# Moving the gate and spill stores to another issuing engine, laying value tiles over finished scratch memory, and starting 92 instead of 79 expert tiles before the gates are done

## The chip, the cores and the metric

The kernel runs on one core of a Trainium2 chip. The metric is the time of one execution on the device, in microseconds (us). PE is the matrix engine (TensorE), DVE is VectorE, ACT is ScalarE, POOL is GpSimd, and SP is SyncE, which here only issues transfers (DMA). Each engine works through its own list of instructions in order; an instruction that waits holds up all that stand behind it on that engine.

## What is computed

The reference is one decoder layer: gated token mixers, and then an expert network (PEER) that takes more than two thirds of the time. Only the second half is touched by the change:

```
def peer(xn, wq, subkeys, u_tab, v_tab):          # 512 tokens, 8 heads, 16 picks a head
    q = (xn @ wq).reshape(bsz, s, PEER_HEADS, 2, PEER_HALF)
    sub = jnp.einsum('bshpd,hpnd->bshpn', q, subkeys)
    s_top, i_top = lax.top_k(sub, PEER_TOPK)       # 16 best of 128 row keys and of 128 column keys
    ...
    best, pos = lax.top_k(cand, PEER_TOPK)         # 16 best of their 256 sums
    expert = jnp.take_along_axis(cand_idx, pos, axis=-1)
    gate = jax.nn.softmax(best, axis=-1)
    ...
    a = gelu(einsum('td,ted->te', xb, u_tab[eb]))
    return einsum('te,ted->td', (gb * a), v_tab[eb])
```

There are 128 x 128 = 16384 experts, each one row of 1024 numbers in the table U and one in the table V.

## The kernel before

The first third of the program (to about 540 us) is the token mixers, the projection to `q` and the search for the best keys. What follows treats the 512 tokens in two ways.

**Dense, for tokens 0 to 383** (three blocks of 128). All 16384 experts are computed, in 128 tiles of 128 experts. An *expert tile* j (`expert_in`) loads a 512 KB tile of U (`wraw`), splits it into a high part (`whi`, cast on ACT) and a low part (`wlo`, subtraction on DVE), multiplies both on PE with the tokens (24 matmuls, `pa`), and applies gelu on ACT. The result (128 experts x 384 tokens, `act`) needs the gates before it can be used. The *gates* are a table of 128 x 384 x 128 numbers, nearly all zero: `choose(b)` finds picks and weights on DVE, then 24 rounds build one-hot tiles on DVE (`jb`, `ib`, `o1`, `o2`) and multiply them on PE (`pg`, 768 products in all), ACT copies the products to `ch`, and 24 stores of 1 MB write them to the memory `gd`. After that the *value loop* runs over j = 0 to 127: a value tile of V is loaded and split like a U tile (`load_w(vt[j], wv, 4)`; four raw tiles, two high and two low ones), a block of gates `gg` (1.5 MB for eight j) is read back from `gd`, DVE multiplies it with `act` (`pr`), ACT and DVE split the product (`ph`, `pl`), and 18 matmuls add to the six sums `y`. Expert tiles that were not done before run between the value tiles.

**Sparse, for tokens 384 to 511.** 128 gathers of U rows (`sparse_in`: POOL gathers, DVE reduces to `dots`) and 128 gathers of V rows (`sparse_out`: DVE adds to `h2l`). Three gather buffers are shared.

Expert tiles do not depend on the gates, so `ahead` runs the first `AHEAD` of them while DVE works on keys and gates. Tiles 0 to 27 stay in SBUF; tiles 28 to AHEAD - 1 are written to the memory `ad` (`actd`, 192 KB each, two buffers) and read back in the value loop. `load_w` has three raw tiles for U and issues its loads on SP. In the kernel before all stores are issued on SP too, and so stand in one list with the loads.

The order on each engine is not that of the code. A scheduler arranges the instructions by its own model before the program is built, and the engines then keep that order whatever the real times are. A pool that is opened after another was closed lies over the closed one's memory, and its first writers wait, tile by tile, for the last users of what lay there.

Of the kernel before, what the change touches and what calls it, by code (L numbers as in the profile page):

```python
# [9 lines left out]
F32 = mybir.dt.float32  # L10
F32R = mybir.dt.float32r
F16 = mybir.dt.float16
# [8 lines left out]
P = 128  # L21
# [39 lines left out]
def kernel(ctx: ExitStack, tc: tile.TileContext, x, pos, cst, wtok, wsm, wcol, wkv, spt,  # L61
                             wab, wo, wq, skt, g1b, g2b, u_rows, ut, v_rows, out, dbg=None):
    nc = tc.nc
    V, G, A, T, SY = nc.vector, nc.gpsimd, nc.scalar, nc.tensor, nc.sync
# [16 lines left out]
    def load_w(src, wp=wp, raws=RAW):  # L81
        raw = wp.tile([P, D], F32, name="wraw", tag="wraw", bufs=raws)
        hi = wp.tile([P, D], F32R, name="whi", tag="whi")
        lo = wp.tile([P, D], F32R, name="wlo", tag="wlo")
        SY.dma_start(raw, src)
        A.copy(hi, raw)  # L86
        V.tensor_tensor(lo, raw, hi.bitcast(F32), ALU.subtract)  # L87
        return hi, lo
# [54 lines left out]
    with ExitStack() as c1:  # L143
# [39 lines left out]
        with tc.tile_pool(name="xin", bufs=4, reuse_waits="tile") as xp:  # L183
# [43 lines left out]
            with tc.tile_pool(name="rp", bufs=1) as rp:  # L227
# [38 lines left out]
                for k, p2 in ((a1, 9), (a2, 20)):  # L266
# [4 lines left out]
                    t = tmp()  # L271
# [351 lines left out]
    TO = 8  # L623
    NCH = ND // TC
    JG = 8
    AHEAD = 79
    KEPT = 28
    EARLY = 2
    GS = 2.0 ** 15
# [12 lines left out]
    def expert_in(j):  # L642

        hi, lo = load_w(ut[j])
        ps = psa.tile([P, S], F32, name="pa", tag="pa")
        expert_mm(ps, hi, lo, 0, ND)
        if KEPT <= j < AHEAD:
            a = spill.tile([P, ND], F32, name="actd")
            A.activation(a, ps[:, :ND], AF.Gelu_apprx_tanh)  # L649
            SY.dma_start(ad[j - KEPT], a)  # L650
            return None
        a = stash.tile([P, ND], F32, name="act")
        A.activation(a, ps[:, :ND], AF.Gelu_apprx_tanh)
        return a
# [31 lines left out]
    with ExitStack() as c2:  # L686
# [6 lines left out]
        iota = kp.tile([P, P], F16, name="iota")  # L693
        V.tensor_copy(iota, iota_i)
        it16 = iota[:, :PK]
        iob = kp.tile([P, TO // 4, P, 4], F16, name="iob")
        V.tensor_copy(iob, iota.unsqueeze(1).unsqueeze(3).to_broadcast([P, TO // 4, P, 4]))

        order = [NB - 1] + list(range(NB - 1))
        top_s = [kp.tile([P, PH, 2, PK], F32, name=f"top_s{b}") for b in range(NB)]  # L700
# [33 lines left out]
                        top16(top_s[b][:, h, p, :], top_i[b][:, h, p, :], subs[p][:, b * P:(b + 1) * P])  # L734

        ks = c2.enter_context(tc.tile_pool(name="ks", bufs=2, reuse_waits="tile"))
        chp = c2.enter_context(tc.tile_pool(name="chp", bufs=2, reuse_waits="tile"))
        oh = c2.enter_context(tc.tile_pool(name="oh", bufs=2, reuse_waits="tile"))

# [60 lines left out]
        for b in range(NB - 1):  # L800
            ahead(2)
            tr = []
            for n, src in enumerate(choose(b)):
                pt = sm.tile([P, S], F32, name="pgt", tag="sm")
                T.transpose(pt[:, :P], src, ident)
                t = ks.tile([P, P], F32 if n == 2 else F16, name=f"tr{n}")
                A.activation(t, pt[:, :P], AF.Copy, scale=GS if n == 2 else 1.0)
                tr.append(t)
            jT, iT, gT = tr[1], tr[0], tr[2]
            ghi = ks.tile([P, P], F16, name="ghi")  # L810
            V.tensor_copy(ghi, gT)
            glo = ks.tile([P, P], F16, name="glo")
            V.tensor_tensor(glo, gT, ghi, ALU.subtract)
            for cc in range(P // TC):
                ch = chp.tile([P, P, TC], F32, name="ch")
                for to in range(0, TC, TO):
                    t0 = cc * TC + to

                    ahead(1)

                    def over(a):
                        return (a[:, t0:t0 + TO].rearrange("p (g u) -> p g u", u=4).unsqueeze(2)
                                .to_broadcast([P, TO // 4, P, 4]))

                    jb, ib, o1, o2 = (oh.tile([P, TO // 4, P, 4], F16, name=n) for n in ("jb", "ib", "o1", "o2"))
                    V.tensor_tensor(jb, iob, over(jT), ALU.is_equal)
                    V.tensor_tensor(ib, iob, over(iT), ALU.is_equal)
                    V.tensor_tensor(o1, ib, over(ghi), ALU.mult)  # L828
                    V.tensor_tensor(o2, ib, over(glo), ALU.mult)
                    for t4 in range(0, TO, 4):  # L830
                        pg = gp.tile([P, 4, P], F32, name="pg")
                        for u in range(4):
                            for o in (o1, o2):
                                T.matmul(pg[:, u, :], jb[:, t4 // 4, :, u], o[:, t4 // 4, :, u], start=o is o1,  # L834
                                         stop=o is o2)
                        A.activation(ch[:, :, to + t4:to + t4 + 4].rearrange("p i t -> p t i"), pg, AF.Copy,  # L836
                                     scale=1.0 / GS)
                SY.dma_start(gd[:, b * (P // TC) + cc], ch)

        ahead(P)  # L840

    with ExitStack() as c3:
        yp = c3.enter_context(tc.tile_pool(name="yp", bufs=1, space=PSUM))
        gr = c3.enter_context(tc.tile_pool(name="gr", bufs=2, reuse_waits="tile"))
        wv = c3.enter_context(tc.tile_pool(name="wv", bufs=2, reuse_waits="tile"))
        cp = c3.enter_context(tc.tile_pool(name="cp", bufs=3, reuse_waits="tile"))
        ys = [[yp.tile([P, 512], F32, name=f"y{b}_{hf}") for hf in range(2)] for b in range(NB - 1)]
        vt = v_rows.rearrange("(i j) d -> i j d", j=P)
# [3 lines left out]
        def feed():  # L852

            done[0] += 1
            while done[1] < n_todo and done[1] * n_load < n_todo * done[0]:
                f, s = todo[done[1]]
                f(s)
                done[1] += 1

        for j in range(P):  # L860
            if j % JG == 0:
                gt = gr.tile([P, NCH, JG, TC], F32, name="gg", tag="gg")
                SY.dma_start(gt, gd[:, :, j:j + JG, :])
                if j + JG == P:
                    hr = gr.tile([P, NB - 1, D], F32, name="hr", tag="gg")
                    SY.dma_start(hr, hd)
            room = max(KEPT - 5 - max(0, KEPT - j), 0) + max(0, j - AHEAD)
            while len(acts) < min(P, AHEAD + min(room, (P - AHEAD) * (j + 1) // (P - 4))):
                acts.append(expert_in(len(acts)))
                feed()  # L870
            if acts[j] is None:
                acts[j] = stash.tile([P, ND], F32, name="act")
                SY.dma_start(acts[j], ad[j - KEPT])
            hi, lo = load_w(vt[j], wv, 4)
            pr = cp.tile([P, ND], F32, name="pr", bufs=2)
            V.tensor_tensor(pr.rearrange("p (c t) -> p c t", c=NCH), acts[j].rearrange("p (c t) -> p c t", c=NCH),
                            gt[:, :, j % JG, :], ALU.mult)
            ph = cp.tile([P, ND], F32R, name="ph")
            pl = cp.tile([P, ND], F32R, name="pl")
            A.copy(ph, pr)  # L880
            V.tensor_tensor(pl, pr, ph.bitcast(F32), ALU.subtract)  # L881
            for b in range(NB - 1):
                bs = slice(b * P, (b + 1) * P)
                for hf in range(2):
                    ds = slice(hf * 512, (hf + 1) * 512)
                    with tc.issue_after(last_mm.ins) if j == P - 1 and (b or hf) else nullcontext():
                        last_mm = mm3(ys[b][hf], ph[:, bs], pl[:, bs], hi[:, ds], lo[:, ds], j == 0, j == P - 1)
            feed()
# [75 lines left out]
```

## Time and profile before

| | us |
|---|---|
| median of three runs | 1670.01 (1667.72 to 1675.47) |
| the profiled execution, its own time | 1667.96 |
| span of its profile | 1666.2 |
| PE busy | 1604.0 (96%) |
| DVE busy | 1274.0 (76%) |
| ACT busy | 647.7 (39%) |

The span runs from the first to the last instruction in the profile; the other 1.8 us lie around it. Busy time counts work alone: an engine that only issues a transfer is not counted as busy for it. "Idle" is always the idle time of one engine, and costs something only where that engine is the one that the end waits for. The share of 96% is an average over the program; the slices and windows below show where the rest is.

### The profile page before, as it was taken

Reading aid. Unit: us, or ns where it says so; the run is one execution under the profiler, and the core shown is the slowest. Engines: PE = TensorE matmul, PEld = TensorE weight load, DVE = VectorE, ACT = ScalarE, POOL = GpSimd, SP = SyncE. Lnnn points to the kernel's source line nnn. Section 1 sums busy time; section 2 is a strip of 40 time slices with the busy share of each in tenths; the row PEclk is TensorE's granted clock in tenths of the full one; section 3 lists DMA queues with packets and bytes.
Section 4 is the critical chain, followed back from the end, with each engine's and each line's share of the span. In section 5 each row is a group of like instructions: output and inputs, shape, how many; then the busy total and the mean of one; then the engine's idle time right before and its main releaser. Section 6 shows DMA issues by size and latency. Waiting matters only on the chain.

```text
span 1666.2 us, 22533 instructions
## 1 busy us (share of the span) xinstructions
PE 1604.0 (96%) x8173; PEld 1400.8 (84%) x8173; DVE 1274.0 (76%) x2670; ACT 647.7 (39%) x954; POOL 357.2 (21%) x280
## 2 busy tenths in 40 slices
PE   8999999999999999999995499999999999999999
PEld 6777768888899999999994488888888888988887
DVE  5599955459999998888888588878788788874543
ACT  5453333332344344555555233333333333333332
POOL 0010000000001442222222233434434234430000
PEclk9999999999999999999995699999999999999999
DMA  5212233222224898889878999999999989985432
GB/s 209 76 51 76 89 136 117 89 102 89 77 102 159 299 323 295 316 278 332 300 280 290 313 314 334 342 350 338 338 344 341 371 309 323 326 317 183 152 126 77
DMA packets 154351, 386.74 MB, mean 232 GB/s; under 512 B 12288, under 2 KB 74496, under 8 KB 150656
## 3 DMA queue, kind: packets, MB, share of 16 engines
q1 hardware_dynamic: 117376, 251.07, 42.6%
q0 software_dynamic: 36864, 134.23, 23.2%
q8 instruction: 64, 1.05, 0.2%
q14 instruction: 47, 0.39, 0.1%
HBM read 346.40 MB, written 38.86 MB: 231 GB/s over the span
## 4 chain that ended last, share of the span: by engine, by line
PE 65%; DVE 12%; DMA 12%; issue 7%; POOL 3%; ACT 1%; SPq 0%; POOLq 0%; DVEq 0%; ACTq 0%
PE pa L93 6%; PE pa L91 6%; PE pa L92 6%; PE y L92 6%; PE y L91 6%; PE y L93 6%; DMA gt<-in_v_rows,eid 5%; PE pg L834 4%; DVE wlo L87 3%; POOL gt L658 3%; PE pcol L92 2%; PE pcol L91 2%; PE pcol L93 2%; PE pq L92 2%; PE pq L91 2%
## 5 line engine op out<-in xcount | busy, mean ns | idle before, releaser
L86 ACT CAST whi<-wraw 128x1024 fp32r<-128x1024 f32 x320 | 335.0, 1053 | 372.8 <-PE pa L92 129.7
L87 DVE TENSOR_TENSOR wlo<-wraw,whi 128x1024 fp32r<-128x1024 f32 x320 | 389.1, 1218 | 95.2 <-ACT whi L86 90.7
L93 PE MATMUL pa<-hh,wlo 128*128 128x384 f32 (+2 forms) x1040 | 350.5, 338 | 1.9 <-DVE wlo L87 1.9
L91 PE MATMUL pa<-hh,whi 128*128 128x384 f32 (+2 forms) x1040 | 350.0, 337 | 0.7 <-ACT actd L649 0.7
L92 PE MATMUL pa<-hl,whi 128*128 128x384 f32 (+2 forms) x1040 | 349.8, 336 | 0.0
L92 PE MATMUL y<-wlo,ph 128*128 128x512 f32 x768 | 299.9, 391 | 0.4 <-DVE wlo L87 0.4
L93 PE MATMUL y<-whi,pl 128*128 128x512 f32 x768 | 296.6, 391 | 0.0
L658 POOL DMA_INDIRECT gt<-in_u_rows,eid x128 | 167.8, 1311 | 530.2 <-DVE dots L664 328.0
L91 PE MATMUL y<-whi,ph 128*128 128x512 f32 x768 | 239.2, 393 | 27.5 <-ACT whi L86 27.4
L658 POOL DMA_INDIRECT gt<-in_v_rows,eid x128 | 177.1, 1383 | 262.9 <-DVE h2l L673 221.6
L880 ACT CAST ph<-pr 128x384 fp32r<-128x384 f32 x128 | 65.4, 514 | 357.7 <-PE y L92 292.8
L93 PEld LDWEIGHTS pa<-hh,wlo 128*128 128x128 f32 x1040 | 196.9, 189 | 5.6 <-DVE wlo L87 3.4
L91 PEld LDWEIGHTS pa<-hh,whi 128*128 128x128 f32 x1040 | 197.0, 189 | 5.0 <-ACT actd L649 1.4
L92 PEld LDWEIGHTS pa<-hl,whi 128*128 128x128 f32 x1040 | 196.8, 189 | 3.3
L673 DVE SCALAR_TENSOR_TENSOR h2l<-gt,coef,h2l 128x1024 f32<-128x1024 f32 x128 | 164.0, 1281 | 42.7 <-DMA gt<-in_v_rows,eid 41.7
L91 PEld LDWEIGHTS y<-whi,ph 128*128 128x128 f32 x768 | 144.2, 189 | 55.3 <-ACT whi L86 28.1
L664 DVE CUSTOM_DVE_ANT_0 gt<-gt,hn 128x1024 f32<-128x1024 f32 x128 | 155.6, 1218 | 33.0 <-DMA gt<-in_u_rows,eid 32.9
L92 PEld LDWEIGHTS y<-wlo,ph 128*128 128x128 f32 x768 | 144.1, 188 | 30.2 <-DVE wlo L87 0.7
L93 PEld LDWEIGHTS y<-whi,pl 128*128 128x128 f32 x768 | 144.2, 188 | 29.3
L881 DVE TENSOR_TENSOR pl<-pr,ph 128x384 fp32r<-128x384 f32 x128 | 70.5, 554 | 96.7 <-ACT ph L880 94.6
L836 ACT ACTIVATE ch<-pg 128x512 f32<-128x512 f32 x96 | 97.1, 1097 | 69.0 <-PE pg L834 63.2
L834 PE MATMUL pg<-o,jb 128*128 128x128 f16 x768 | 104.6, 296 | 12.4 <-DVE o L828 9.9
(305 smaller groups left out, 1977.4 us busy)
## 6 DMA issues: line engine op xcount, KB each, us to landing
wraw<-in_ut SPq DMA_DIRECT2D x128, 512.0 KB
wraw<-in_v_rows SPq DMA_DIRECT2D x128, 512.0 KB
gd<-ch SPq DMA_DIRECT2D x24, 1024.0 KB
gg<-gd SPq DMA_DIRECT2D x16, 1536.0 KB
wraw<-in_wcol SPq DMA_DIRECT2D x20, 512.0 KB
ad<-actd SPq DMA_DIRECT2D x51, 192.0 KB
act<-ad SPq DMA_DIRECT2D x51, 192.0 KB
wraw<-in_wq SPq DMA_DIRECT2D x16, 512.0 KB
```

Source lines behind the costliest of these rows:

```text
L86: A.copy(hi, raw)
L87: V.tensor_tensor(lo, raw, hi.bitcast(F32), ALU.subtract)
L91: T.matmul(ps, lh, rh, start=start, stop=False)
L92: T.matmul(ps, lh, rl, start=False, stop=False)
L93: return T.matmul(ps, ll, rh, start=False, stop=stop)
L658: G.indirect_dma_start(out=t, out_offset=None, in_=table, in_offset=bass.IndirectOffsetOnAxis(ap=eid[:, s:s + 1], axis=0))
L664: V.tensor_tensor_reduce(out=t, in0=t, in1=hn3, scale=1.0, scalar=0.0, op0=ALU.mult, op1=ALU.add, accum_out=dots[:, s:s + 1])
L673: V.scalar_tensor_tensor(h2l, t, coef[:, s:s + 1], h2l, ALU.mult, ALU.add)
L834: T.matmul(pg[:, u, :], jb[:, t4 // 4, :, u], o[:, t4 // 4, :, u], start=o is o1, stop=o is o2)
L836: A.activation(ch[:, :, to + t4:to + t4 + 4].rearrange("p i t -> p t i"), pg, AF.Copy, scale=1.0 / GS)
L880: A.copy(ph, pr)
L881: V.tensor_tensor(pl, pr, ph.bitcast(F32), ALU.subtract)
```

## The change

Three things are changed. The stores of `gd` and of `ad` are issued by ACT, the engine that wrote what they store, and no longer by SP. The memory is laid out anew: what the 24 rounds still need (`tr`, `ghi`, `glo`, `iob`) moves from the pools `ks` and `kp` to a pool `gs` of its own, and the value pool `wv` is opened ahead of the gate pool `gr`, so that it lies over `kp` and `ks`, which are done when the last `choose` is. The value tiles are loaded by `load_v`, which is called for tiles 0 and 1 ahead of the loop. And `AHEAD` is 92, so that 64 instead of 51 tiles are written to `ad` and read back, and 36 instead of 49 are left for the value loop.

```diff
-    AHEAD = 79
+    AHEAD = 92
...
             A.activation(a, ps[:, :ND], AF.Gelu_apprx_tanh)
-            SY.dma_start(ad[j - KEPT], a)
+            A.dma_start(ad[j - KEPT], a)
...
-        iob = kp.tile([P, TO // 4, P, 4], F16, name="iob")
-        V.tensor_copy(iob, iota.unsqueeze(1).unsqueeze(3).to_broadcast([P, TO // 4, P, 4]))
...
         ks = c2.enter_context(tc.tile_pool(name="ks", bufs=2, reuse_waits="tile"))
+        gs = c2.enter_context(tc.tile_pool(name="gs", bufs=2, reuse_waits="tile"))
+        iob = gs.tile([P, TO // 4, P, 4], F16, name="iob", bufs=1)
+        V.tensor_copy(iob, iota.unsqueeze(1).unsqueeze(3).to_broadcast([P, TO // 4, P, 4]))
...
-                t = ks.tile([P, P], F32 if n == 2 else F16, name=f"tr{n}")
+                t = gs.tile([P, P], F32 if n == 2 else F16, name=f"tr{n}")
...
-            ghi = ks.tile([P, P], F16, name="ghi")
+            ghi = gs.tile([P, P], F16, name="ghi")
...
-            glo = ks.tile([P, P], F16, name="glo")
+            glo = gs.tile([P, P], F16, name="glo")
...
-                SY.dma_start(gd[:, b * (P // TC) + cc], ch)
+                A.dma_start(gd[:, b * (P // TC) + cc], ch)
...
+        wv = c3.enter_context(tc.tile_pool(name="wv", bufs=2, reuse_waits="tile"))
         gr = c3.enter_context(tc.tile_pool(name="gr", bufs=2, reuse_waits="tile"))
-        wv = c3.enter_context(tc.tile_pool(name="wv", bufs=2, reuse_waits="tile"))
...
+        vq = []
+
+        def load_v(n):
+            while len(vq) < min(n, P):
+                vq.append(load_w(vt[len(vq)], wv, 4))
+
+        load_v(2)
         for j in range(P):
...
-            hi, lo = load_w(vt[j], wv, 4)
+            load_v(j + 1)
+            hi, lo = vq[j]
```

What this does to the order is seen at the hand-over from the gates to the value loop. The numbers in the names below are buffer numbers, which the two programs give out differently.

SP, before: the last stores of gates (`gd`), the first block of gates read back (`gg`) and the first value tiles (`in_v_rows`). The loads of U in it are tiles 86 and 87.

```order
L838 DMA gd_3137<-ch_7067 128x2048
L85 DMA wraw_9625<-in_ut 128x1024
L838 DMA gd_3137<-ch_7196 128x2048
L85 DMA wraw_9730<-in_ut 128x1024
L838 DMA gd_3137<-ch_7325 128x2048
L838 DMA gd_3137<-ch_7454 128x2048
L838 DMA gd_3137<-ch_7583 128x2048
L838 DMA gd_3137<-ch_7712 128x2048
L863 DMA gg_8682<-gd_3137 128x24x128
L85 DMA wraw_8684<-in_v_rows 128x1024
L85 DMA wraw_8720<-in_v_rows 128x1024
```

SP, now, at the same place: loads of U tiles 94 to 99 (`wraw_9569` to `wraw_10339`), the first two value tiles, the gates.

```order
L85 DMA wraw_9569<-in_ut 128x1024
L85 DMA wraw_9709<-in_ut 128x1024
L85 DMA wraw_9885<-in_ut 128x1024
L85 DMA wraw_10023<-in_ut 128x1024
L85 DMA wraw_10201<-in_ut 128x1024
L85 DMA wraw_10339<-in_ut 128x1024
L85 DMA wraw_9149<-in_v_rows 128x1024
L85 DMA wraw_9155<-in_v_rows 128x1024
L871 DMA gg_9161<-gd_3137 128x24x128
L85 DMA wraw_9222<-in_v_rows 128x1024
L85 DMA wraw_9255<-in_v_rows 128x1024
```

No store is left on SP, two value tiles stand ahead of `gg`, and all of them stand behind the load of U tile 99.

ACT, before, at the same place: the last copies of gate products, then the first products of the value loop.

```order
L836 ACTIVATE ch_7712<-pg_7755 128x4x128
L836 ACTIVATE ch_7712<-pg_7765 128x4x128
L836 ACTIVATE ch_7712<-pg_7820 128x4x128
L836 ACTIVATE ch_7712<-pg_7830 128x4x128
L880 CAST ph_8692<-pr_8690 128x384
L880 CAST ph_8728<-pr_8726 128x384
L86 CAST whi_8685<-wraw_8684 128x1024
```

ACT, now: the last copies, the stores among them, the casts of U tiles 94 to 97 (`whi_9570` to `whi_10024`), those of value tiles 0 and 1, the first product.

```order
L837 ACTIVATE ch_7715<-pg_7833 128x4x128
L650 DMA ad_3149<-actd_9084 128x384
L839 DMA gd_3137<-ch_7715 128x2048
L86 CAST whi_9570<-wraw_9569 128x1024
L649 ACTIVATE actd_9118<-pa_9093 128x384
L653 ACTIVATE act_9388<-pa_9363 128x384
L650 DMA ad_3149<-actd_9118 128x384
L86 CAST whi_9710<-wraw_9709 128x1024
L86 CAST whi_9886<-wraw_9885 128x1024
L86 CAST whi_10024<-wraw_10023 128x1024
L86 CAST whi_9150<-wraw_9149 128x1024
L86 CAST whi_9156<-wraw_9155 128x1024
```

Before, nothing stood between the last gates and the first product `ph`; now four casts of U tiles and two of value tiles do (`ph` is the next row).

DVE, now: the last low parts of U tiles with reductions of gathered rows (`gt`, the `ISA` rows) between them, then value tiles 0 and 1 and the first product. Before, the rows there were seven such reductions and then `pr`.

```order
L87 TENSOR_TENSOR wlo_9887<-wraw_9885,whi_9886 128x1024
L664 ISA gt_10333,dots_3142<-gt_10333,hn3_2653 128x1024
L664 ISA dots_3142 128x1
L87 TENSOR_TENSOR wlo_10025<-wraw_10023,whi_10024 128x1024
L664 ISA gt_10336,dots_3142<-gt_10336,hn3_2653 128x1024
L664 ISA dots_3142 128x1
L664 ISA gt_10372,dots_3142<-gt_10372,hn3_2653 128x1024
L664 ISA dots_3142 128x1
L87 TENSOR_TENSOR wlo_9151<-wraw_9149,whi_9150 128x1024
L87 TENSOR_TENSOR wlo_9157<-wraw_9155,whi_9156 128x1024
L885 TENSOR_TENSOR pr_9163<-act0_3126,gg_9161 128x384
```

The low part of tile 96, the first row, is what sets free the raw tile that the load of tile 99 fills.

On PE the rows are too alike to be shown, so here are their counts. Before, the last expert tile ahead of the gates' end is number 81 (counted from 0): 24 matmuls, then 176 of the 768 gate products in one stretch, then `y`. Now expert tiles stand between the gate products to their end: after the last product follow the last 20 matmuls of tile 91, tiles 92, 93 and 94 whole, and then `y`.

## Rows read from the trace of the kernel before

**Rows 1.** The page, 40 slices of 41.7 us: busy tenths of PE, granted clock.

```profile
PE   8999999999999999999995499999999999999999
...
PEclk9999999999999999999995699999999999999999
```

**Rows 2.** Busy time by stretch: PE, PEld, DVE, ACT, POOL, clock, DMA share, GB/s.

```profile
600.00:875.50 275.50, 273.59 (x1746) 261.53 (x1745) 234.46 (x349) 141.37 (x176) 75.79 (x57) 0.99 0.86 304
875.50:911.20 35.70, 23.67 (x177) 19.63 (x176) 33.15 (x56) 21.21 (x23) 9.44 (x9) 0.59 0.86 298
911.20:938.20 27.00, 0.02 (x1) 0.02 (x1) 9.50 (x19) 3.22 (x6) 7.80 (x7) 0.50 0.92 318
938.20:944.00 5.80, 5.80 (x17) 5.22 (x18) 4.49 (x6) 2.06 (x4) 0.94 (x1) 0.53 1.00 289
938.20:1500.00 561.80, 560.85 (x2641) 486.54 (x2642) 454.94 (x538) 197.79 (x275) 216.19 (x162) 1.00 0.95 333
1200.00:1300.00 100.00, 100.00 (x466) 85.68 (x465) 80.03 (x90) 34.33 (x47) 39.83 (x26) 1.00 0.99 345
```

**Rows 3.** PE in order of time: start, length, what, idle before.

```profile
869.50 1.95 PE L834 MATMUL pg<-o,jb 128*128 128x128 f16 x15
871.20 0.42 PE L91 MATMUL pa<-hh,whi 128*128 128x384 f32 x1
...
875.47 2.19 PE L834 MATMUL pg<-o,jb 128*128 128x128 f16 x17
...
909.36 1.80 PE L834 MATMUL pg<-o,jb 128*128 128x128 f16 x14 [0.20 <-DVE o L829]
938.18 2.07 PE L91 MATMUL y<-whi,ph 128*128 128x512 f32 x4 [27.02 <-ACT whi L86]
```

**Rows 4.** The chain of work that ended last, at the hand-over: start, length, what.

```profile
910.38 1.96 ACT ch L836 x2
...
912.36 8.03 DMA gd<-ch
...
920.60 0.61 SPq L863
...
921.30 15.68 DMA wraw<-in_v_rows
```

**Rows 5.** DVE and ACT in order of time at the hand-over.

```profile
933.74 1.23 DVE L664 CUSTOM_DVE_ANT_0 gt<-gt,hn 128x1024 f32<-128x1024 f32 x1 [9.66 <-DMA gt<-in_u_rows,eid]
...
934.89 1.02 DVE L876 TENSOR_TENSOR pr<-act,gg 128x384 f32<-128x384 f32 x2
...
935.48 0.98 ACT L880 CAST ph<-pr 128x384 fp32r<-128x384 f32 x2 [23.15 <-DVE pr L876]
```

**Rows 6.** Groups by shape, 700 to 860 us: busy us, mean ns, idle before.

```profile
L664 DVE CUSTOM_DVE_ANT_0 gt<-gt,hn 128x1024 f32<-128x1024 f32 x32 | 39.0, 1218 | 0.0
...
L87 DVE TENSOR_TENSOR wlo<-wraw,whi 128x1024 fp32r<-128x1024 f32 x27 | 33.0, 1222 | 14.5 <-ACT whi L86 14.5
L86 ACT CAST whi<-wraw 128x1024 fp32r<-128x1024 f32 x27 | 28.6, 1059 | 17.5 <-PE pa L92 15.2 <-DVE o L828 1.5 <-DMA wraw<-in_ut 0.7
L828 DVE TENSOR_TENSOR o<-ib,ghi 128x1024 f16<-128x1024 f16 x24 | 16.5, 686 | 0.2 <-PE pg L834 0.2
```

**Rows 7.** What SP's list waited for, 480 to 960 us: total us, times, longest.

```profile
SPq L650 <- ACT actd L649: 140.2, 46, 6.8
SPq L838 <- ACT ch L836: 91.1, 22, 10.1
```

**Rows 8.** Issue of stores on SP: shortest, median and longest in ns.

```profile
L838 SPq DMA_DIRECT2D gd<-ch x24: 319/323/574, 619.4 to 912.4; - x24
L650 SPq DMA_DIRECT2D ad<-actd x51: 319/320/1123, 579.4 to 857.9; - x51
```

**Rows 9.** Issues of single loads on SP, in order of time: start, length.

```profile
921.30 5.19 SPq L85 DMA_DIRECT2D wraw<-in_v_rows  x1
...
975.66 0.33 SPq L85 DMA_DIRECT2D wraw<-in_v_rows  x1
```

## Prediction

> **What bounds the kernel now.** I read the slices first [rows 1]: PE is at nine tenths or more nearly everywhere, so the kernel is bound by PE, but for two slices around 920 to 1000 us, where both its busy share and its clock fall to about half. The windows cut that hole more finely [rows 2]. From 600 to 875.5 PE works 273.6 of 275.5 us. From 875.5 to 911.2 it works 23.7 of 35.7 us while DVE works 33.2: DVE's one-hot tiles are the bound there. From 911.2 to 938.2 PE does nothing. After 938.2 PE is full again, with the transfers at 333 GB/s and a share of 0.95. So 39 us of PE are lost in one place, and the rest of the program is PE's own work.
>
> The order in time says why [rows 3]. At 875.47 us the last expert tile that stands ahead of the gates' end is through, number 81, and 176 gate products are left, which DVE doles out until 911.16. The chain of waits then names the second part [rows 4]: two copies on ACT, 8.03 us until the last gate store has landed, the issue of the gate block on SP, and 15.68 us for the value tile behind it. DVE and ACT show that the gate block was no later than 934.89, where the first product `pr` starts, directly behind a reduction that had waited 9.66 us for a gather [rows 5].
>
> **The change, part by part.** *The stores leave SP.* SP's list stood 231 us behind stores that waited for ACT [rows 7], but PE waited for no U tile there (1.9 us idle in 275.5, [rows 2]); this gives nothing by itself. On ACT the 88 stores (24 and 64) cost issue time that no row shows for that engine. The nearest are SP's: a median of 0.32 us, at most 1.12 [rows 8]; that makes 28 to 99 us. ACT is idle for 134 of the 275.5 us of the gate stage [rows 2], and the stage grows by 23 us (below), so the work is covered. I take 0; the cover is gone at about 1.7 us a store (rival 3).
>
> *`iob` is built later.* One DVE copy of 1024 columns a partition (the nearest row is 0.69 us, [rows 6]) moves into the key search. I take 0; it costs at most that.
>
> *13 more tiles run ahead.* In the built order, PE has 91 whole tiles and 4 matmuls of tile 91 ahead of the last gate product; before it had 82. Tile 81 takes from 871.20 to 875.47, its first matmul longer than the rest for the gate products ahead of it [rows 3]; I take 4.2 us a tile, 0.175 a matmul. A gate product is 1.70/15 = 0.113 us when PE does not wait (869.50 to 871.20, [rows 3]). If PE sets the pace, the last gate product ends at 875.5 + 9 x 4.2 + 0.7 + 176 x 0.113 = T = 933.9 us. Does DVE allow that? For the last eight of the 24 x 2 pieces it has 32 one-hot operations of 0.69 us, 7 low parts and 8 reductions of 1.22 us [rows 6], 40 us; PE has 7 tiles and 128 products, 44 us. So PE is the bound, and the 12 us of waiting before 911 go, with the half clock. I add 1 us for waits in order, between 0 and 5.
>
> Behind T, PE has 92 more matmuls, 16.1 us, so its work lasts to 950.0, with 95 tiles done in place of 82.
>
> *The hand-over.* Here the value tiles and gates do not come early, although their memory is free. On SP they stand behind the load of U tile 99, and that needs the raw tile of tile 96, which DVE gives up after `wlo` of 96, which needs `whi` of 96, which needs the high tile of 93, which PE holds to the end of 93. That is T + 68 x 0.175 = 945.8; 1.06 us of cast and 1.22 of subtraction [rows 6] and three issues of 0.33 us with gaps [rows 9] put the issue of `gg` at 949.3. Its store landed by then (T + 2.0 + 8.0 = 943.9, [rows 4]). From issue to `pr` it took 14.3 us before (920.60 to 934.89, [rows 4, 5]); this time 1.5 MB of loads lie ahead of it, but no reduction that waits 9.66 us. At 318 GB/s [rows 2] the loads are 4.9 us. I take 14.3, and 14.3 + 4.9 as the upper bound. Then `pr` and `ph`, half a microsecond each [rows 5]: `y` starts at 964.7. PE is idle for about 15 us instead of 27.
>
> The lower bound is the chain that holds even if the gates had landed: after tile 94 ends at 950.0, cast and low part of tile 97 (1.06 + 1.22), two reductions and two low parts of value tiles (4 x 1.22), `pr` and `ph` (1.0): 958.2. The upper one is 969.6.
>
> *The value loop* has 13 tiles less, 54.6 us of PE. Its transfers stay. By the order, between j = 4 and j = 112 stand 134 loads and 160 gathers of 512 KB, 64 tiles of 192 KB read back and 13.5 gate blocks of 1.5 MB, 188 MB; before, from j = 4 to 104, 136 loads, 165 gathers, 51 and 12.5, 187 MB, and PE needed 562 us for these [rows 2], 4.13 us a load. So now 188 MB go into 553 us, 340 GB/s in place of 333. PE was full at 345 from 1200 to 1300 [rows 2], at a share of 0.99. I take 1.5 us of waits; the upper bound is 12 (rival 2).
>
> **The sum** is made against the profiled execution, 1667.96 us (2.0 under the median of the runs). `y` starts 26.5 us later (964.7 against 938.2) with 54.6 us less to do: 28.1 us gained. Less 1 in the gates and 1.5 in the loop: 25.6, so **1642 us**. The clock I leave out: before, it came back only after `y` had begun (four matmuls in 2.07 us, [rows 3]), at a clock of 0.53 in the first 5.8 us [rows 2]; a hole of 15 us may bring that again. If it does not, 5.8 x 0.47 = 2.7 us more are saved.
>
> **The rivals.**
>
> 1. *The gates come in time* and the hand-over is only the 8.2 us of its own chain, because the stores have left SP's queue and the gathers are few. For it: the 14.3 us contain the wait for a gather [rows 5]. Against: 3 MB of loads and gates at 318 GB/s are 9.9 us after 948.5 or so. Time: `y` at 958.2, 34.6 gained, less 2.5: 1636 us, and 1631 with all waits gone and the clock up.
>
> 2. *The transfers become the bound of the value loop.* For it: the share is 0.95 already [rows 2], and the density rises. If the mean of 333 GB/s were all there is, 188 MB would take 565 us, 12 above 553. Against: the 345 of the fullest window [rows 2]. Time of the rival: 1642 + 12 - 1.5, about 1653 us.
>
> 3. *ACT becomes the bound, and the kernel is slower.* The stores stand between the casts that PE needs. ACT's free time in the gate stage is 134 us and about 20 more in the longer stage; 88 stores use it up at 1.7 us each. From there each tenth costs 8.8 us, so the gain is gone at 2.0 us a store. For it: a load issued right behind a gate block took 5.19 us on SP [rows 9], and at that price ACT would be 300 us over, some 1940 us. Against: that is the issue behind `gg`, of which there is none in the gate stage, and the 75 stores before stayed at 0.32 in the median [rows 8]. [...]
>
> 4. *The gain is not there*: DVE paces the gates after all, and the wait at the hand-over is as long as it was. If T comes 5 us later and `y` starts 27 us after 955, it is at 982, and 10.8 us are left of the gain, 1657; with 12 lost in the loop it is 1669, no change.
>
> **How the numbers follow.** The forecast (1637 to 1650) has 0.60, rival 1 0.14, rival 2 0.15, rival 3 0.04, rival 4 0.07. The likeliest time is 1642. The range reaches down to rival 1 with everything in its favour, 1631, and up to the upper bounds of the hand-over and the loop together (969.6, and 12 in the loop: 54.6 - 31.4 - 1 - 12 = 10.2 us gained), 1658. That leaves out rival 3, half of rival 4 and the tails of the others, some 2 in 10. A measurement of this kernel tells 0.5% from no change, 8.4 us: below 1661.7 is faster. The forecast and rivals 1 and 2 lie there, and half of rival 4: faster 0.91, same 0.05, slower 0.04.
>
> **What the profile will show.** If I am right: the slices around 880 to 930 at nine tenths; the last gate product near 934; tile 94 ending near 950; `gg` issued on SP about 15 us after the last gate product, right behind the load of tile 99; one hole of PE of about 15 us, ended by `ph` or by a cast of value tile 0; `y` from about 965; PE at 99% after that with about 340 GB/s. If the hole is 8 us and is ended by DVE's chain, rival 1 holds. If PE shows waits for `whi` or `wlo` between 1050 and 1450 with a DMA share of 1.0, rival 2. If ACT shows long issues and PE waits for `whi` in the gate stage, rival 3. What would make the prediction wrong is above all the landing time of `gg`, which is taken from one row, and the assumption that the order's counts become PE's pace.

## The result and the profile after

The changed kernel takes 1645.7 us (median of four executions, 1643.72 to 1650.58); the kernel before, run beside it, takes 1670.37 (1667.72 to 1675.47). The ratio is 0.9859, 95% interval 0.9834 to 0.9884, so it is faster, clear of the noise. The forecast was 1642 with a range of 1631 to 1658. Of all executions reported here one, of the kernel without read-back (3998 us), was far slower than its fellows and is left out of its range and ratio. The execution profiled takes 1647.18 us, its span is 1645.5: 20.7 us less span than before, where 25.6 were forecast.

The slices of the changed kernel, in tenths of 40 slices, answer to [rows 1].

```profile
PE   8999999999999999999999959999999999999999
...
PEclk9999999999999999999999979999999999999999
```

One slice is left with a hole in it, the 41 us from 946 on. The windows cut it out, and show the loop behind it.

```profile
core 0: us, PE busy (x) PEld busy (x) DVE busy (x) ACT busy (x) POOL busy (x), PEclk, DMA share, GB/s
600.00:900.00 300.00, 300.00 (x1939) 288.41 (x1938) 256.35 (x382) 160.46 (x200) 77.60 (x61) 1.00 0.87 307
900.00:945.60 45.60, 45.60 (x293) 43.67 (x291) 29.64 (x43) 23.15 (x27) 8.28 (x9) 1.00 0.85 301
945.60:963.90 18.30, 0.20 (x2) 0.00 (x0) 7.00 (x10) 3.69 (x5) 4.00 (x3) 0.62 1.02 337
963.90:970.00 6.10, 6.09 (x20) 4.91 (x21) 3.17 (x7) 2.39 (x6) 0.00 (x0) 0.73 1.13 313
...
1065.00:1095.00 30.00, 26.16 (x112) 21.40 (x111) 21.76 (x33) 8.40 (x12) 9.23 (x8) 0.94 0.94 326
...
963.90:1645.50 681.60, 671.67 (x3096) 573.17 (x3096) 513.50 (x621) 230.75 (x321) 203.76 (x162) 1.00 0.85 300
```

Beside [rows 2]: PE does not miss a tenth of a microsecond from 600 to 945.6, so the 12 us in which DVE doled out gate products are gone. One hole of 18.1 us stands where one of 27.0 stood. Between 1065 and 1095, inside the value loop, 3.84 us are lost that nothing before answers to.

The timeline of PE around the hole: start, length, what, and in brackets the idle time and what ended it.

```profile
928.74 1.11 PE L835 MATMUL pg<-o,jb 128*128 128x128 f16 x8
963.91 0.79 PE L91 MATMUL y<-whi,ph 128*128 128x512 f32 x1 [18.11 <-ACT ph L889]
```

The timeline of SP, with its issues.

```profile
929.44 14.73 SPq L85 DMA_DIRECT2D wraw<-in_ut  x4
944.22 1.15 SPq L85 DMA_DIRECT2D wraw<-in_v_rows  x2
945.46 1.36 SPq L871 DMA_DIRECT2D gg<-gd  x1
946.87 10.14 SPq L85 DMA_DIRECT2D wraw<-in_v_rows  x2
```

And DVE's, where the first product of the value stage stands.

```profile
962.75 1.03 DVE L885 TENSOR_TENSOR pr<-act,gg 128x384 f32<-128x384 f32 x2 [7.77 <-DMA gg<-gd]
```

The chain is the forecast's, link by link. The last gate product ends at 929.85. The block `gg` is issued at 945.46, behind the last of the U tiles' loads and two value tiles. `pr` starts 17.3 us later, after waiting 7.77 us for that block and nothing else. `ph` and `y` follow. Value tile 0 was no hindrance: `ph`, not `whi`, ended the wait.

The stores that went to ACT, grouped by tile: count, and shortest, median and longest issue in ns, beside [rows 8].

```profile
L839 ACTq DMA_DIRECT2D gd<-ch x24: 326/326/327, 618.8 to 931.0; - x24
L650 ACTq DMA_DIRECT2D ad<-actd x64: 326/326/347, 579.7 to 937.6; - x64
```

They cost 0.326 us each, much as on SP (0.32).

### The profile page after: what moved, and what is told of

It is laid out like the page before. It is cut to its first block, busy times and chain, and to the rows that moved or that the text cites. A ratio compares the mean times of both kernels' runs of the same rounds, so it can differ in the third digit from the quotient of the medians.

```text
span 1645.5 us, 22570 instructions
## 1 busy us (share of the span) xinstructions
PE 1600.6 (97%) x8173; PEld 1397.9 (85%) x8173; DVE 1273.2 (77%) x2670; ACT 648.6 (39%) x954; POOL 341.2 (21%) x280
## 3 DMA queue, kind: packets, MB, share of 16 engines
q8 instruction: 64, 1.05, 0.2%
## 4 chain that ended last, share of the span: by engine, by line
PE 72%; issue 13%; DMA 7%; POOL 4%; DVE 3%; ACT 0%; SPq 0%; POOLq 0%; DVEq 0%; ACTq 0%
PE pa L93 8%; PE pa L92 8%; PE pa L91 8%; PE y L92 7%; PE y L93 7%; PE y L91 7%; POOL gt L658 4%; PE pg L835 3%; DMA gt<-in_v_rows,eid 3%; PE pcol L91 2%; PE pcol L92 2%; PE pcol L93 2%; PE pq L91 2%; PE pq L93 2%; PE pq L92 2%
## 5 line engine op out<-in xcount | busy, mean ns | idle before, releaser
L91 PE MATMUL y<-whi,ph 128*128 128x512 f32 x768 | 219.9, 393 | 18.1 <-ACT ph L889 18.1
L658 POOL DMA_INDIRECT gt<-in_v_rows,eid x128 | 162.6, 1271 | 294.0 <-DVE h2l L673 264.1
```

The lines of the kernel that those rows point to most:

```text
L91: T.matmul(ps, lh, rh, start=start, stop=False)
L658: G.indirect_dma_start(out=t, out_offset=None, in_=table, in_offset=bass.IndirectOffsetOnAxis(ap=eid[:, s:s + 1], axis=0))
```

## The experiments

The theory after this result: the 13 tiles are the whole gain, since they are PE work laid under DVE's one-hot tiles and under the wait for the first gate block; stores and layout only place things differently at the hand-over. The rivals: the stores' new engine or the layout bring part of the gain; or the time of the hand-over is set by something other than the landing of `gg`. The first four kernels divide the change, and ran beside a before of 1668.33 us.

**Tiles only**: the kernel before, one number changed.

```
-    AHEAD = 79
+    AHEAD = 92
```

> The kernel before with 92 tiles run ahead; stores stay on SP, the memory as before. Theory A (the 13 tiles are the whole gain: PE had nothing to do while DVE made the gates): 1636 to 1650 us, ratio about 0.983; PE full until after the last gate product, one hole of 10 to 20 us at the hand-over. In this order the gate block stands behind the load of tile 98, not 99, one tile earlier than in the changed kernel, so theory A with the chain that I read (gate block waits on SP behind loads of U that wait for PE) even expects y to begin 3 to 6 us earlier than the 963.9 of the changed kernel, about 1641. Theory B (the tiles need the stores off SP, since 64 stores that wait for ACT hold up the loads): PE shows waits for whi or wlo in the gate stage, 1655 us or more.

Measured: 1641.15 us (1639.36 to 1647.25), ratio 0.9852 (0.9826 to 0.9879). That is the whole gain of the change, and its ratio cannot be told from the full change's. `gg` is issued at 941.19 and `y` starts at 960.8, 3.1 us earlier than in the full change, as expected. Theory B's sign is absent: ahead of the hand-over PE waits 0.3 us for a low part of a U tile and for no high part.

**Stores and layout without the tiles**: the changed kernel with the old number.

```
-    AHEAD = 92
+    AHEAD = 79
```

> The changed kernel with 79 tiles ahead: stores on ACT, value tiles over the scratch memory and loaded ahead of the gate block. Theory A: the gates stay bound by DVE until about 911, the gate block still waits for the last gate store (to about 920) and takes 13 to 17 us; only the value tile behind it is saved: y begins 2 to 4 us earlier than 938.2, 1664 to 1669 us, no change that 0.5% can tell. Theory B (moving stores and value tiles is a good part of the gain): 1658 us or less.

Measured: 1666.8 us (1662.13 to 1672.59), ratio 0.9992 (0.9972 to 1.0012): nothing. The list of what PE waited for there, 600 to 1000 us (total, times, longest), shows both of the old losses back.

```profile
PE y L91 <- ACT ph L889: 21.9, 1, 21.9
PE pg L835 <- DVE o L829: 10.8, 4, 3.8
```

PE waits 10.8 us for DVE's one-hot tiles in the gates and 21.9 for the hand-over, whichever engine issues the stores. One part of theory A missed: in the profiled execution the last gate product ends at 906.29 and `y` starts at 928.20, 10.0 us earlier than before and not 2 to 4. More than half of that is lost again behind it: from the first `y` to the end it takes 733.6 us, where the kernel before takes 728.0, and PE waits there 2.8 us for `wlo` and 2.6 for `ph` (0.4 and 0.2 before).

**Tiles and stores, without the layout**: the kernel before with these edits.

```
-    AHEAD = 79
+    AHEAD = 92
...
-            SY.dma_start(ad[j - KEPT], a)
+            A.dma_start(ad[j - KEPT], a)
...
-                SY.dma_start(gd[:, b * (P // TC) + cc], ch)
+                A.dma_start(gd[:, b * (P // TC) + cc], ch)
```

> The kernel before with 92 tiles ahead and the stores on ACT, memory as before. In this order the gate block stands on SP behind tile 98 and ahead of the value tiles. Theory A with the chain on SP: gate block issued near 940 instead of 945.5, y near 958, 1638 to 1645 us: as fast as the changed kernel or some 5 us faster. Rival (the value tiles over the scratch are what shortens the hole from 27 to 18 us): y near 970 or later, 1650 us or more.

Measured: 1637.24 us (1634.77 to 1639.58), ratio 0.9821 (0.9803 to 0.984), 0.8 us under the theory's lower end; `y` starts at 957.90, as expected.

**Tiles and layout, with the stores back on SP**: the changed kernel with the last two edits reversed.

```
-            A.dma_start(ad[j - KEPT], a)
+            SY.dma_start(ad[j - KEPT], a)
...
-                A.dma_start(gd[:, b * (P // TC) + cc], ch)
+                SY.dma_start(gd[:, b * (P // TC) + cc], ch)
```

> The changed kernel with its stores back on SP. In this order the gate block stands behind tile 98 and two value tiles. Theory A: stores on SP cost nothing that PE sees; gate block issued near 941, y near 959, 1639 to 1647 us. Theory B: PE waits in the gate stage, 1655 us or more.

Measured: 1640.5 us (1637.3 to 1642.15), ratio 0.983 (0.981 to 0.985), as expected; `gg` is issued at 943.41 and `y` starts at 960.53, each some 2 us later than expected. So four kernels with 92 tiles lie between 1637 and 1646, and the one with 79 at 1667. Of the four the full change has the highest median, but all intervals overlap with its own, that of tiles and stores, without the layout, least. The issue of the gate block on SP and the first `y` in that kernel (tiles and stores) show where its lead begins. First SP's timeline.

```profile
940.46 0.61 SPq L863 DMA_DIRECT2D gg<-gd  x1
941.12 9.87 SPq L85 DMA_DIRECT2D wraw<-in_v_rows  x4
```

Then PE's.

```profile
957.90 2.50 PE L91 MATMUL y<-whi,ph 128*128 128x512 f32 x5 [12.38 <-ACT whi L86]
```

There `gg` stands ahead of the load of tile 99 and is issued 5 us earlier than in the full change; `y` starts 6 us earlier. That is half of the 12.4 us between the two profiled executions; the other half lies in the value loop (below). The full change puts `gg` behind the load of tile 99, as the forecast had read from the order. It is not the layout alone that does so: with the layout and the stores on SP, `gg` stands behind tile 98 and two value tiles.

**The first gate block issued by ACT**: the changed kernel with one line. ACT is free at that point, and SP's list is not. This one, the first one with 95 tiles and the last two of this section ran beside a before of 1669.94 us.

```
-                SY.dma_start(gt, gd[:, :, j:j + JG, :])
+                (A if j == 0 else SY).dma_start(gt, gd[:, :, j:j + JG, :])
```

> The changed kernel with one edit: the first gate block is loaded by ACT's list and not by SP's, so it no longer stands behind the loads of U tiles 95 to 99 and of two value tiles. On ACT it stands behind the cast of U tile 96. Theory (the hole of 18 us is made by the place of the gate block in SP's list, which waits for PE, plus some 14 to 17 us of landing): issued near 943 instead of 945.5, with no loads ahead of it in its own queue, landing 12 to 15 us later; y near 956 to 959 instead of 963.9, 1638 to 1642 us. Rival (the landing time is contention of all that is in flight, so that an earlier issue lands no earlier): y at 962 or later, 1644 us or more.

Measured: 1651.17 us (1649.33 to 1654.96), ratio 0.989 (0.9851 to 0.9928): a miss, 9 us above the upper end. The block was issued 4.4 us earlier, and landed 3 us later. ACT's timeline has the issue and the cast of value tile 0.

```profile
941.07 0.59 ACTq L871 DMA_DIRECT2D gg<-gd  x1
...
956.83 1.04 ACT L86 CAST whi<-wraw 128x1024 fp32r<-128x1024 f32 x1 [10.56 <-DMA wraw<-in_v_rows]
```

SP's shows what it issued in the meantime.

```profile
943.82 5.43 SPq L85 DMA_DIRECT2D wraw<-in_v_rows  x4
949.35 0.61 SPq L871 DMA_DIRECT2D gg<-gd  x1
```

DVE's shows when the block was there.

```profile
965.91 1.03 DVE L885 TENSOR_TENSOR pr<-act,gg 128x384 f32<-128x384 f32 x2 [6.78 <-DMA gg<-gd]
```

In the changed kernel, SP's issue of value tiles 2 and 3 stands for 10.14 us behind `gg`, and the second block is issued behind them at 957.11. With the block on ACT's queue, SP issues four value tiles in 5.43 us and a second block behind them, 3.5 MB by 949.96, and value tile 0 lands late too: its cast starts at 956.83, in the changed kernel at 950.01. From issue to `pr` it is 24.8 us in place of 17.3. In both kernels the transfers were full over that stretch (a share of 1.04 at 340 GB/s from 945 to 970 here, 1.01 at 337 from issue to use in the changed kernel). Value tile 0, issued at 943.82 behind the block, had landed by 956.83, while DVE waited for the block until 965.91; so what was issued behind the block was moved beside it, and the block, issued 4.4 us earlier by its new place in a list, took 7.5 us longer to be used.

**95 tiles**: tiles and stores as above, with 95.

```
-    AHEAD = 92
+    AHEAD = 95
```

> As the run with tiles and stores alone (memory as before, stores on ACT), with 95 in place of 92 tiles ahead. The order puts two more expert tiles, 97 instead of 95, ahead of y and leaves the gate block behind tile 98 on SP. Theory (the hole is a wait that more tiles can fill at no cost up to its length): PE's work lasts to about 954, y begins 958 to 963, 1630 to 1635 us. Rival (three more tiles to write and read back, 1.2 MB, and a fuller value loop give it back as waits of PE): 1637 us or more.

Measured: 1634.23 us (1629.56 to 1634.79), ratio 0.9774 (0.9736 to 0.9812), as expected in time; but `y` starts at 965.2, later than expected, and three tiles are 12.4 us, of which 3.0 were gained over 92 by the medians, 8 by the ratios. ACT's timeline shows a wait that was not expected.

```profile
942.45 0.49 ACT L649 ACTIVATE actd<-pa 128x384 f32<-128x384 f32 x1 [0.40 <-ACT actd L649]
956.61 0.33 ACTq L650 DMA_DIRECT2D ad<-actd  x1
957.05 1.99 ACT L86 CAST whi<-wraw 128x1024 fp32r<-128x1024 f32 x2 [14.11 <-DMA gg<-gd]
958.95 0.48 ACT L653 ACTIVATE act<-pa 128x384 f32<-128x384 f32 x1
```

The spill store of one tile has its data at 942.9 and is issued at 956.61, the moment `gg` lands. Its place in the program's order, with the semaphores that it waits on, and that of the first `pr` on DVE:

```
650 L650 DMA ad_3149<-actd_9186 128x384 [waits DMAHW5_49,Activation_49]
1577 L876 TENSOR_TENSOR pr_9258<-act0_3126,gg_9250 128x384 [waits DMAHW5_49]
```

Both wait on DMAHW5: `pr`, which reads the gate block, and the store, which does not and was issued only when the block had landed, 13.7 us after its own data were there. Behind the store stand two casts and the activation that empties PSUM (the memory that PE writes its sums to) for the next tile, and PE waited 8.8 us for that activation.

**95 tiles, all stores on SP**: the kernel before, with only the number. This kernel and the two after it ran beside a before of 1666.74 us.

```
-    AHEAD = 79
+    AHEAD = 95
```

> The kernel before with AHEAD = 95 and nothing else: 95 tiles ahead as in the last run but one on this point (95 tiles, stores by ScalarE, 1634.2 us), but every store issued by SyncE. In that run ScalarE stood from 942.9 to 956.6 us with a spill store whose semaphore is shared with the first gate block's transfer, and behind it stood the activation that frees the PSUM buffer of the next tile, so that TensorE's tile 96 began only at 959.49. Theory (the held store cost the gap): with the store on SyncE tile 96 runs in the gap, the gap ahead of y is under 4 us, y starts at 959 to 962, and the time is 1628 to 1632 us. Rival (the gap is only the wait for the gate block, wherever the store stands; SyncE's stores cost again the 4 us by which tiles alone stood above tiles with ScalarE's stores): 1634 to 1639.

Measured: 1631.11 us (1628.64 to 1632.82), ratio 0.9771 (0.9744 to 0.9798), inside the theory's bounds. What PE waited for, 900 to 1650 us.

```profile
PE y L92 <- DVE wlo L87: 3.5, 1, 3.5
PE pa L91 <- ACT actd L649: 2.7, 2, 1.3
PE pa L91 <- ACT act L653: 1.3, 1, 1.3
PE y L91 <- ACT ph L880: 0.4, 1, 0.4
```

There is no gap ahead of `y` any more beyond 0.4 us, and 1.3 us three times at a tile. So the held store was the cause of the gap. It cost less than its 8.8 us, for `y` needs the gate block all the same: `pr` starts at 957.99 and `y` at 961.5, only 3.7 us earlier than with the held store, and from there to the end it takes 1.8 us longer (669.3 us, 667.5 with the held store). In time the two kernels with 95 tiles cannot be told apart; their ratios are 0.9771 and 0.9774.

**The full change with 96 tiles**: one number.

```
-    AHEAD = 92
+    AHEAD = 96
```

> The changed kernel with AHEAD = 96 in place of 92. Theory (the 18.1 us gap ahead of y is TensorE time that four more tiles of 4.2 us fill while the first gate block is on its way; y still starts at about 964): 16 us less than the changed kernel, 1628 to 1633 us, and the gap ahead of y falls under 4 us. Rival (the gap comes back in another form: the spill stores of the four tiles stand on ScalarE behind the gate block's transfer and keep PSUM from coming free, as with 95 tiles and the old layout): 8 to 10 us stay idle ahead of y, and the time is 1636 to 1642.

Measured: 1624.38 us (1622.58 to 1633.23), ratio 0.9753 (0.9715 to 0.9791), the fastest kernel of this study by its median, under the change with 92 by 21 us by the medians and 18 by the ratios. All that PE waited for in it from 600 to 1620 us:

```profile
PE y L91 <- ACT ph L889: 1.5, 1, 1.5
PE y L92 <- DVE wlo L87: 1.4, 2, 0.9
PE pa L91 <- ACT actd L649: 1.3, 1, 1.3
PE pa L91 <- ACT act L653: 1.3, 1, 1.3
```

From the first `y` to the end:

```profile
960.00:1620.90 660.90, 655.38 (x3024) 558.54 (x3024) 511.66 (x619) 227.93 (x316) 208.72 (x162) 1.00 0.89 312
```

The hole of 18.1 us is filled up to 1.5, so it was room for tiles. The steps are not quite the theory's. The order puts three more tiles ahead of `y`, not four: 72 matmuls fewer are left behind it (3024, 3096 in the changed kernel), 12.4 us. And `y` starts at 960.0 and not at 964, since `gg` is issued at 942.78, 2.7 us earlier, and used after 16.1 us. Here no store is held by the block: the first `pr` waits on DMAHW1 and starts at 958.84; the two stores issued after the block wait on 5 and 7 and go out at 944.12 and 947.43. The two profiled spans are 24.6 us apart, and 12.4 and 3.9 us of that are these two steps. The other 8.3 lie in the loop and brought the median 4 us under the theory's lower end: PE's waits for `wlo` fell from 5.6 to 1.4 us, and the granted clock stays at 1.00 from the first `y` to 1619, where the changed kernel has 0.73 in the first 6.1 us and falls once more in the loop.

**98 tiles**, in the old layout with ACT's stores.

```
-    AHEAD = 92
+    AHEAD = 98
```

> The kernel before with ScalarE's stores and AHEAD = 98. With 95 tiles of it the time was 1634.2 and TensorE stood idle for some 10 us ahead of y. Theory (only tiles that fit between the last gate product and y's start are worth time; the program hands over y's first products ahead of tile 96 here): no further gain over 95 tiles, 1631 to 1637 us, and up to 2 us more for three more stores and read-backs. Rival (each further tile ahead is still worth its 4.1 us): 1620 to 1624.

Measured: 1639.73 us (1637.48 to 1643.9), ratio 0.983 (0.98 to 0.986), 2.7 us above the theory's 1637, 0.7 with the 2 us that it allowed for stores and read-backs, and far above its rival. ACT's timeline has the same held store, this time ahead of the cast of value tile 0.

```profile
958.33 0.33 ACTq L650 DMA_DIRECT2D ad<-actd  x1
958.78 1.99 ACT L86 CAST whi<-wraw 128x1024 fp32r<-128x1024 f32 x2 [12.81 <-DMA gg<-gd]
```

PE's timeline: `y` waits for that cast.

```profile
963.56 2.93 PE L91 MATMUL y<-whi,ph 128*128 128x512 f32 x6 [9.84 <-ACT whi L86]
```

The order puts `y` ahead of tile 96 here, so that the tiles past 95 no longer lie under the wait. They bring nothing, and the wait is paid.

**No read-back**: the changed kernel, in which the spilled activations are not read again and all those tiles use the first activation instead.

```
-                acts[j] = stash.tile([P, ND], F32, name="act")
-                SY.dma_start(acts[j], ad[j - KEPT])
+                acts[j] = acts[0]
```

> The changed kernel without the 64 reads of spilled tiles: the products take tile 0 in their place, so the output is not the layer's. 12.6 MB less in the value loop; up to its start the order is the same. y begins at 964 as in the changed kernel. Theory (what the loop lost beyond the forecast, about 6 us, is DVE waiting in its list for gathers and read-backs that land late in a transfer system that is nearly full): the waits of PE for wlo go from 5.6 to under 2 us, 1638 to 1642 us. Rival (the loss is in the loop's order or in PE's own pace): 1644 us or more.

Measured: 1664.73 us (1651.38 to 1669.57), ratio 0.9946 (0.9917 to 0.9976): a miss, and in the other direction. With 12.6 MB less to move, the kernel got 19 us slower by the medians, some 15 by the ratios. DVE's waits there from 1040 to 1500 us:

```profile
DVE h2l L673 <- DMA gt<-in_v_rows,eid: 66.9, 47, 7.0
DVE gt L664 <- DMA gt<-in_u_rows,eid: 13.8, 8, 4.9
```

The same two waits in the changed kernel:

```profile
DVE h2l L673 <- DMA gt<-in_v_rows,eid: 16.9, 15, 3.1
DVE gt L664 <- DMA gt<-in_u_rows,eid: 15.2, 6, 5.3
```

PE's waits for `wlo` rose from 5.6 us to 15.8. Without the reads the program's order is another one: it puts the gathers of V rows closer together (they start between 1089.8 and 1492.5, in the changed kernel between 1088.1 and 1541.9), DVE comes to many of them before their data have landed, and the low parts that PE needs stand behind. So this run changes the order along with the bytes, and does not price the bytes by themselves; it shows that the place of the gathers in DVE's list can cost the loop more than 12.6 MB less give back.

**Each read-back twice**, in the changed kernel.

```
                 SY.dma_start(acts[j], ad[j - KEPT])
+                SY.dma_start(acts[j], ad[j - KEPT])
```

> The changed kernel with each of the 64 reads of spilled tiles done twice, 12.6 MB more in the value loop; nothing else differs up to its start. If the transfers bound the loop at about 350 GB/s, 553 us carry 194 MB and the 188 + 13 MB need some 20 us more: 1660 us or more, or less if the end of the loop, where the share falls to 0.4, takes it up. If there is room, the gathers end some 35 us later and PE waits little: 1645 to 1652 us.

Measured: 1656.94 us (1653.45 to 1663.75), ratio 0.9925 (0.9895 to 0.9955), between the expectations. From 1050 to 1500 us the traffic was 340 GB/s at a share of 0.97, against 333 at 0.94, and PE worked 444.45 us in place of 445.38. The spans of the two profiled executions are 6.3 us apart, and 3.8 of these lie behind 1500 us, where PE is idle for 9.1 us in place of 5.3 while the gathers run on. So the loop's transfers have some room; how much of the 11 us between the medians is bytes and how much the order, this run does not tell.

## Why the prediction was right, and where its sizes were off

**The mechanism held at each step up to the first `y`.** The tiles fill the gates: PE is full from 600 to 945.6. The stores cost ACT nothing that PE sees (rival 3 needed 2.0 us a store; it was 0.326, 28.7 us for 88). Five of the 88 stores overlap an issue on SP, by 0.02 to 0.20 us (one is issued at 775.17, the load at 775.04); both sides took 0.33 us, and no wait shows. The hand-over has the forecast chain, behind the load of tile 99, and ends with `ph`. Stores and layout bring nothing by themselves in time, as costed, though in the profiled execution of that kernel `y` began 10 us earlier and the loop took 5.6 longer; that the tiles are the gain is shown by the first two experiments. Rival 1, that the gates come in time, did not happen; rival 4, that DVE paces the gates, did not either. One reading was off: the two slices with the hole in [rows 1] are those from 875 to 958 us, not 920 to 1000; the windows that the prediction goes on with are right.

**Three terms were mis-sized; two nearly cancel.** T, the last gate product, came at 929.85 and not 933.9. Of these 4 us, 1.9 are PE's idle time ahead of 875.5 that I had left standing [rows 2], and 0.4 to 0.6 are the tile's price: 4.16 us by the 92 matmuls behind T, 4.13 by PE's busy time (below), instead of 4.2, nine times. The rest I have not split. The 1 us added for waits in the gates did not come. PE's work behind T lasted 16.0 us, forecast 16.1, and `gg` was issued 3.8 us early. Its landing took 17.3 us where I had taken 14.3, within the bound of 19.2. All kernels with 92 to 98 tiles in which SP issues it lie between 14.0 and 17.7 (14.0 in tiles and stores, 17.0 in tiles only, 16.1 in the full change with 96; in the two with a held store counted to its release). So the one row of before was the fast end of this, and the middle would have been the better choice. `y` started at 963.91, forecast 964.7.

**The third term is the one that made the forecast too low, by 4 us in the median and 4.9 in the span: the waits in the value loop.** From the first `y` to the end the span fell from 728.0 to 681.6 us, 46.4, and not by 54.6 less 1.5. The windows of three kernels over just that stretch account for it. The kernel before:

```profile
938.20:1666.20 728.00, 723.29 (x3408) 627.25 (x3408) 530.04 (x632) 250.00 (x347) 216.19 (x162) 1.00 0.82 287
```

Tiles and stores without the layout:

```profile
957.90:1633.10 675.20, 669.67 (x3096) 572.03 (x3096) 515.45 (x621) 231.98 (x321) 204.17 (x163) 1.00 0.88 305
```

Both that kernel and the changed one (681.60, 671.67, shown above) run 312 matmuls fewer, 13 tiles. Without the layout PE's busy time falls by 53.6 us: a tile is 4.13 us, 1.0 us less over the 13 than I took (the clock's earlier return at the first `y` is contained in it: its matmuls are at their full pace 3.3 us after the first `y`; in the kernel before, the clock was 0.50 for the first 4.8 us). In the changed kernel it falls by 51.6: the same work took 2.0 us longer. The granted clock explains most of it: 0.94 between 1065 and 1095, where it falls behind the second of two waits; eight matmuls of `y` from 1090.03 on follow each other at 0.43 us in place of 0.23, which is 1.6 us. PE's idle time rises from 4.7 to 9.9 us, 5.2 more, and that is PE's wait for `wlo` in the loop, 0.4 us before and 5.6 now (total, times, longest).

```profile
PE y L92 <- DVE wlo L87: 0.4, 1, 0.4
PE y L92 <- DVE wlo L87: 5.6, 4, 2.4
```

The sum closes: 1.0 + 2.0 + 5.2 = 8.2 = 54.6 - 46.4. So 7.2 us of the 8.2 are waits and the clock behind them, where I had 1.5; my bound was 12.

Were these the transfers (rival 2)? The place and the tile waited for are the ones that the prediction gave as its sign: PE waits for `wlo` at 1070 and 1089.

```profile
1070.36 0.50 PE L92 MATMUL y<-wlo,ph 128*128 128x512 f32 x1 [1.46 <-DVE wlo L87]
1089.47 0.50 PE L92 MATMUL y<-wlo,ph 128*128 128x512 f32 x1 [2.38 <-DVE wlo L87]
```

But the share from 1065 to 1095 is 0.94, not 1.0. DVE's waits in that stretch say more.

```profile
1067.47 1.23 DVE L664 CUSTOM_DVE_ANT_0 gt<-gt,hn 128x1024 f32<-128x1024 f32 x1 [3.33 <-DMA gt<-in_u_rows,eid]
1085.02 1.23 DVE L664 CUSTOM_DVE_ANT_0 gt<-gt,hn 128x1024 f32<-128x1024 f32 x1 [5.28 <-DMA gt<-in_u_rows,eid]
```

DVE stands 3.3 and 5.3 us before a reduction whose gather has not landed, and the low part that PE needs is behind it. While it stood, the share was 0.84 the first time and 1.05, at 387 GB/s, the second time, with a gate block issued at 1070.80 on its way. So at the second wait a burst of transfers is likely part of the cause. Over the whole loop their amount is not the bound: tiles and stores has the same 13 tiles and keeps PE busy for 529.91 of the 530 us from 970 to 1500, and the full change with 96 tiles, whose loop is denser, for 530.00. What differs is the order, in which a gather can stand too close to its use, and the runs point to the one that comes with the layout and 92 tiles. PE waits 5.6 us for `wlo` in the full change, 4.0 with the stores back on SP and 6.1 with the first block from ACT, against 0.6 and 1.3 in tiles only and in tiles and stores. The layout with 96 tiles has 1.4, so the layout alone is not the cause, and what in the order makes it so stays open.

**The clock** did come back late once more (0.73 in the first 6.1 us of `y`, 0.53 in 5.8 us before), as left open.

## What to carry to other kernels

When the bounding engine stands at a hand-over, count the independent work that it could be given there and set that number by the gap that the next profile shows: here four more than the change's 92 were worth another 18 to 21 us, 12.4 of them by the three tiles that came to stand ahead of the first `y`, and tiles that the order no longer places there brought nothing. Which engine issues a transfer matters less for its 0.33 us than for what stands behind it: a store that waited on the gate block's semaphore stopped ACT, and every cast behind it, for 13.7 us. Before a load is moved to a free queue to start sooner, look at what its old place was holding back; here that let the block land sooner (used 17.3 us after its issue, 24.8 when ACT issued it).

## What the runs showed of the hardware

A store issued by ACT took 0.326 us, by SP 0.32. A store on ACT and a load on SP whose issues overlapped, by 0.02 to 0.20 us, did not lengthen each other: 0.33 us each in all five cases in the changed kernel. SP stood long at loads right behind a 1.5 MB gate block: 10.14 us for two, 9.87 for four, while the block was on its way. This spaced the transfers: where the block came from ACT's queue, SP issued four loads in 5.43 us, and the block took 24.8 us instead of 14.0 to 17.7 to be used. A wait of PE as short as 2.38 us within the loop was followed by a fall of the granted clock (0.51 from 1090 to 1092 and 0.64 from 1092 to 1094), while behind one of 1.46 us it stayed at 1.00. The 5.2 us of waits added in the loop came with 2.0 us more of PE's busy time for the same matmuls, an estimated 1.6 of them from that fall (eight matmuls at 0.43 us in place of 0.23).
